# Matmul with bias and residual: the head loaded in smaller alternating pieces, the tail stored in another order

## The chip, the cores and the metric

The kernel runs on one core of a Trainium2 chip. A core has a matrix engine (TensorE, "PE" in the profile; its weight loads are "PEld"), VectorE ("DVE"), ScalarE ("ACT"), GpSimd ("POOL") and SyncE ("SP"), which here only issues transfers. Sixteen DMA engines move data between the device memory and the on-chip memory. The metric is the device time of one execution in microseconds (us). Before the change it is 211.38 us (median of 7 runs, 211.16 to 211.61). Profile times count from the span's start.

## The reference

```python
def setup_inputs():
    batch, m, k, n = 16, 512, 1024, 768
    # all standard normal, float32
    # x (batch, m, k), weight (k, n), bias (n,), residual (batch, m, n)

def reference(x, weight, bias, residual):
    return (np.matmul(x, weight) + bias + residual).astype(np.float32)
```

There are 8192 rows. x is 33.6 MB, residual and output are 25.2 MB each, weight is 3.1 MB.

## The kernel before

**Tiles.** The 8192 rows are cut into 64 tiles t of 128 rows and 8 super tiles S of 8 tiles (`J = 8`). In a super tile, partition p holds eight consecutive rows of memory, one for each of its tiles; so a transfer of tiles j0 to j1 of S is 128 rows of (j1 - j0) x 4096 bytes for x, or (j1 - j0) x 3072 bytes for the residual and the output.

**Buffers.** x has two super tile buffers (`X_SLOTS`), so x of S may be loaded when the casts of S - 2 are done. The residual has four (`RO_SLOTS`); the result is formed in place in the residual's buffer and stored from there, so the residual of S may be loaded when the store of S - 4 has landed. The weight is staged in residual buffer 1, so the residual of S1 has to wait for the casts of the weight. The first six tiles use buffer 3 for interim sums (`TMP_SLOT`, `EARLY_END`), so the residual of S3 waits until GpSimd has added those.

**One tile.** ScalarE (in the head also VectorE) casts a tile of x to bf16 (line 146; 143 and 144 where two engines share a tile). TensorE transposes it, two bf16 values taken as one fp32 word (line 154), VectorE copies the transposed tile out of PSUM (line 155), and 16 matmuls of 512 or 256 columns (line 161) make 128 x 768 sums in one of three PSUM buffers (`HEAD`). VectorE adds the residual to them (line 196, `finish`). The bias has been added to the residual by GpSimd beforehand (line 186, `pool_adds`). For tiles 0 to 5 it is the other way round: VectorE adds the bias to the sums (line 192), and GpSimd adds that to the residual later (line 182).

**Order of the work.** All engines run their instructions in the order in which the program gives them (`keep_in_program_order`). `HEAD_ORDER` is the head up to tile 2. The main loop does, for t from 3 to 63: cast of t + 2, transposes and PSUM copy of t + 1, matmuls of t, finish of t - 1. On VectorE the copy of t + 2 thus stands behind the finish of t - 1, and the matmuls of t + 2 can't begin before either is done. `ADDS` is a list of preference for GpSimd: `pool_adds(upto)` goes through it and emits those with t up to `upto`, but stops at the first whose data isn't there yet in program order. For the given list the order comes out as 0, 1, 2, 3, 6, 4, 7, 5, 8, 9 and on by number.

**Transfers.** All transfers are issued by SyncE, on one queue, in the order of the list `ORDER`. An entry is (kind, S, j0, j1): x, w (weight), b (bias), r (residual), s (store), c (store of one column chunk of the last tile). `pump()` goes through the list and stops at an entry whose producers haven't been emitted; SyncE then waits at run time for what the entry depends on. Each transfer also uses one of eight semaphores in turn, so it waits for the landing of the transfer issued eight before it. An entry of kind s may carry a fifth number, at which it is cut by partitions into two transfers (`edges`, line 125); no entry of the list before has one. The end of the list:

```python
 ('r', 7, 0, 8), ('s', 4, 0, 8), ('s', 5, 0, 8), ('s', 6, 0, 8), ('s', 7, 0, 5), ('s', 7, 5, 7),
 ('c', 7, 7, 0), ('c', 7, 7, 1)]
```

**Tail.** The last tile's matmuls (line 255) go chunk by chunk, 512 columns and then 256, each in a PSUM buffer of its own, each added (line 259) and stored by itself.

Of the kernel before, what the change touches and what calls it, by code (L numbers as in the profile page):

```python
# [16 lines left out]
HEAD = 3  # L17
XT_N = 4
# [1 line left out]
WARM = 12  # L20
EARLY_END = 6
TMP_SLOT = {0: 3}
ADDS = [6, 0, 7, 8, 1, 9, 2, 10, 3, 11, 4, 12, 5, 13, 14, 15]
HEAD_ORDER = [('cast', 0, 'v'), ('cast', 1, 's'), ('tr', 0), ('tr', 1), ('wc', 0, 0, 's'), ('wc', 0, 1, 'g'),
# [5 lines left out]
ORDER = [('x', 0, 0, 2), ('w', 0, 0, 2), ('x', 0, 2, 4), ('w', 1, 0, 2), ('b', 0, 0, 0), ('w', 2, 0, 2),  # L30
# [6 lines left out]


@with_exitstack
def kernel(  # L40
# [8 lines left out]
    nc = tc.nc  # L49
# [4 lines left out]
    N = weight.shape[1]  # L54
# [3 lines left out]
    chunks = [(0, 512), (512, N - 512)]  # L58
# [9 lines left out]
    def fixed(pool, name, n, shape, dt):  # L68
        return [pool.tile(shape, dt, name=f"{name}", tag=f"{name}{i}", bufs=1) for i in range(n)]
# [4 lines left out]
    XT = fixed(sb, "xt", XT_N, [P, n_q, P, 2], BF16)  # L74
    PO = fixed(ps, "psum_o", HEAD, [P, N], FP32)
# [7 lines left out]
    K_ = tc.keep_in_program_order  # L83
# [5 lines left out]
    def pump():  # L89
        while queue:  # L90
            kind, S, j0, j1, *cut = queue[0]
            if kind == "c":
                need = [("outc", j1)]
            elif kind in ("w", "b"):
                need = []
            elif kind == "x":
                need = [("cast", J * (S - X_SLOTS) + j) for j in range(j0, j1)] if S >= X_SLOTS else []
            elif kind == "r":
                need = [("store", S - RO_SLOTS, j) for j in range(j0, j1)] if S >= RO_SLOTS else []
                if S == 1:  # L100
                    need = [("wcast", n_q - 1)]
                if S in TMP_SLOT.values():
                    need = [("add", t) for t in range(EARLY_END) if TMP_SLOT[t // J] == S]
            else:
                need = [("out", J * S + j) for j in range(j0, j1)]
            if not all(n in done for n in need):
                return
            queue.pop(0)
            if kind == "b":
                K_(nc.sync.dma_start(  # L110
                    out=bias_row.rearrange("(g p) n -> g p n", p=QUAD)[:, 0, :],
                    in_=bias[None, :].to_broadcast([P // QUAD, N]),
                ))
                continue
            if kind == "w":
                K_(nc.sync.dma_start(out=w_st[:, 2 * S + j0:2 * S + j1, :], in_=w_d[:, S, j0:j1, :]))  # L116
                continue
            if kind == "x":
                K_(nc.sync.dma_start(out=X[S % X_SLOTS][:, j0:j1, :], in_=x_d[S, :, j0:j1, :]))  # L119
            elif kind == "r":  # L120
                K_(nc.sync.dma_start(out=R[S % RO_SLOTS][:, j0:j1, :], in_=res_d[S, :, j0:j1, :]))
            else:
                n0, nl = (0, N) if kind == "s" else chunks[j1]
                j1 = j1 if kind == "s" else j0 + 1
                edges = [0, *cut, P]
                for p0, p1 in zip(edges, edges[1:]):
                    K_(nc.sync.dma_start(
                        out=out_d[S, p0:p1, j0:j1, n0:n0 + nl],
                        in_=R[S % RO_SLOTS][p0:p1, j0:j1, n0:n0 + nl],
                    ))  # L130
                done.update(("store", S, j) for j in range(j0, j1))
            done.update((kind, J * S + j) for j in range(j0, j1))

    def mark(*what):
        done.add(what)
        pump()
# [30 lines left out]
    def row(t, n0=0, nl=N):  # L167
        return R[t // J % RO_SLOTS][:, t % J, n0:n0 + nl]
# [3 lines left out]

    adds = list(ADDS) + list(range(max(ADDS) + 1, n_t))

# [32 lines left out]
    def bias_rows():  # L207
        K_(nc.vector.stream_shuffle(out=bias_sb, in_=bias_row, mask=[0] * QUAD))

    pump()  # L210
    for kind, *a in HEAD_ORDER:
        if kind == "bias":
# [10 lines left out]
        elif kind == "wc":  # L223
            q, e, eng = a
# [4 lines left out]
        else:  # L229
            for e in range(2):  # L230
                for n0, nl in chunks:
                    mm(a[0], n0, nl, a[1], e)
    pump()
    for t in range(HEAD - 1):
        if ("fin", t) not in done:
# [12 lines left out]
        finish(t - 1)  # L248
        pool_adds(t + 1)
    t = n_t - 1  # L250
    tail = [(PO[t % HEAD], 0, 512), (PO[(t - 2) % HEAD], 512, N - 512)]
    for p, n0, nl in tail:
        for q in range(n_q):
            for e in range(2):
                K_(nc.tensor.matmul(  # L255
                    p[:, 0:nl], lhsT=XT[t % XT_N][:, q, :, e], rhs=w_sb[:, q, e, n0:n0 + nl],
                    start=(q == 0 and e == 0), stop=(q == n_q - 1 and e == 1),
                ))
        K_(nc.vector.tensor_add(out=row(t, n0, nl), in0=p[:, 0:nl], in1=row(t, n0, nl)))  # L259
        mark("outc", chunks.index((n0, nl)))  # L260
    mark("out", t)
    pump()
    assert not queue, queue
# [30 lines left out]
```

## Time and profile before

| | us |
|---|---|
| median of 7 runs | 211.38 (211.16 to 211.61) |
| the profiled execution | 211.59 |
| its span, first to last instruction | 209.80 |
| PE busy | 201.5 (96%) |
| POOL busy | 116.1 (55%) |
| DVE busy | 104.7 (50%) |
| ACT busy | 67.7 (32%) |
| DMA engines, share of the main queue | 97.6% |
| moved in all | 87.24 MB, 416 GB/s on the mean |

How to read it: a busy time is that of one engine's instructions; the share is of the span. The DMA share is the mean over sixteen engines. The chain of waits is followed back from the last instruction to what released each step. A transfer has landed when all its parts have: its data is spread over the DMA engines, and each of these marks the end of its own part, so that a transfer of 128 rows leaves sixteen marks in the trace. Single DMA packets are recorded too, with start, duration and size. The granted TensorE clock was 0.998 over the span.

### The profile page before, as it was taken

The numbers are of one execution on the slowest core, as the hardware profiler recorded it, in microseconds if no ns is written. First come the engines' busy times: TensorE is split into PE (matmuls) and PEld (weight loads), VectorE is DVE, ScalarE is ACT, GpSimd is POOL, SyncE is SP. The second block draws the span as 40 slices with busy tenths as digits, with TensorE's granted clock in tenths as the row PEclk, the third lists the DMA queues.
The fourth block names the chain that finished last, engine by engine and source line by source line (L and its number), as shares of the span: only waits on it lengthen the run. The fifth ranks groups of instructions, "written<-read, shape, count | busy, mean of one in ns | idle before, by whom it ended". The sixth has DMA issues, their size and how long they took to land.

```text
span 209.8 us, 3119 instructions
## 1 busy us (share of the span) xinstructions
PE 201.5 (96%) x1298; PEld 129.8 (62%) x1298; DVE 104.7 (50%) x140; ACT 67.7 (32%) x69; POOL 116.1 (55%) x72
## 2 busy tenths in 40 slices
PE   7799997999999999999999999999999999999991
PEld 2455655666666666666666666666666666666651
DVE  0558542465275445455544554455455445544542
ACT  2444207060733053323432152330633133321000
POOL 2100099995278980199599702994069910699000
PEclk9999999999999999999999999999999999999999
DMA  6999999999999999999999999999999999999785
GB/s 243 425 424 435 427 416 443 449 406 414 460 440 401 417 445 434 401 475 394 439 444 433 433 408 431 420 453 409 450 422 440 419 422 439 431 436 423 322 378 231
DMA packets 5350, 87.24 MB, mean 416 GB/s; under 512 B 596, under 2 KB 724, under 8 KB 1496
## 3 DMA queue, kind: packets, MB, share of 16 engines
q1 hardware_dynamic: 5336, 87.05, 97.6%
q8 instruction: 10, 0.16, 0.3%
q14 instruction: 4, 0.03, 0.0%
HBM read 61.88 MB, written 25.17 MB: 415 GB/s over the span
## 4 chain that ended last, share of the span: by engine, by line
PE 82%; DMA 14%; ACT 1%; SPq 0%; DVE 0%; issue 0%; ACTq 0%
PE psum_o L161 69%; DMA x_tile<-in_x_dram 14%; PE pt L154 12%; PE psum_o L255 1%; ACT xb L146 1%; DVE ro L259 0%; SPq L116 0%; SPq L119 0%; ACTq L146 0%
## 5 line engine op out<-in xcount | busy, mean ns | idle before, releaser
L161 PE MATMUL psum_o<-w_sb,xt 128*128 128x512 bf16 x1008 | 174.0, 326 | 0.5 <-DVE xt L155 0.3
L161 PEld LDWEIGHTS <-xt 128*128 128x128 bf16 x1008 | 98.5, 98 | 59.2 <-DVE xt L155 0.7
L186 POOL TENSOR_TENSOR ro<-ro,bias_sb 128x768 f32<-128x768 f32 x58 | 103.3, 1824 | 53.8 <-DMA ro<-in_residual_dram 53.8
L146 ACT CAST xb<-x_tile 128x1024 bf16<-128x1024 f32 x60 | 61.3, 1044 | 113.8 <-PE pt L154 57.0
L155 DVE COPY xt<-pt 128x1024 bf16<-128x1024 bf16 x64 | 44.0, 690 | 77.1 <-PE pt L154 77.1
L196 DVE TENSOR_TENSOR ro<-psum_o,ro 128x768 f32<-128x768 f32 x57 | 54.1, 950 | 13.6 <-POOL ro L186 12.5
L154 PE MATMUL pt<-ident,xb 128*128 128x128 f32 x256 | 38.4, 274 | 2.4 <-ACT xb L146 1.3
L154 PEld LDWEIGHTS pt<-ident,xb 128*128 128x128 f32 x256 | 29.6, 140 | 11.3 <-ACT xb L146 2.0
L182 POOL TENSOR_TENSOR ro<-ro 128x768 f32<-128x768 f32 x6 | 10.7, 1808 | 18.5 <-DMA ro<-in_residual_dram 18.5
L192 DVE TENSOR_TENSOR ro<-psum_o,bias_sb 128x768 f32<-128x768 f32 x6 | 5.6, 948 | 0.0
L205 PE MATMUL psum_o<-warm 128*128 128x512 bf16 x12 | 4.2, 521 | 1.2 <-DVE warm_a L201 1.2
L226 ACT CAST w_sb<-ro 128x768 bf16<-128x768 f32 x4 | 3.3, 832 | 3.7 <-DMA ro<-in_weight_dram 3.7
L226 POOL CAST w_sb<-ro 128x768 bf16<-128x768 f32 x1 | 0.8, 824 | 5.3 <-DMA ro<-in_weight_dram 5.3
L205 PEld LDWEIGHTS <-warm 128*128 128x128 bf16 x12 | 1.4, 126 | 3.5 <-issue 1.9
L143 ACT CAST xb<-x_tile 128x512 bf16<-128x512 f32 x3 | 1.8, 617 | 3.4 <-PE psum_o L161 1.7
L146 DVE CAST xb<-x_tile 128x1024 bf16<-128x1024 f32 x1 | 0.7, 693 | 4.3 <-DMA x_tile<-in_x_dram 4.3
L255 PE MATMUL psum_o<-w_sb,xt 128*128 128x512 bf16 (+1 forms) x16 | 2.8, 326 | 0.0
L226 DVE CAST w_sb<-ro 128x768 bf16<-128x768 f32 x3 | 1.7, 557 | 2.0 <-DMA ro<-in_weight_dram 2.0
L144 DVE CAST xb<-x_tile 128x512 bf16<-128x512 f32 x3 | 1.2, 425 | 2.6 <-DMA x_tile<-in_x_dram 2.6
L255 PEld LDWEIGHTS <-xt 128*128 128x128 bf16 x16 | 1.6, 98 | 1.1
L220 PE MATMUL psum_o<-warm 128*128 128x512 bf16 x6 | 1.6, 379 | 0.0
L259 DVE TENSOR_TENSOR ro<-psum_o,ro 128x512 f32<-128x512 f32 (+1 forms) x2 | 1.1, 558 | 0.9 <-PE psum_o L255 0.8
(14 smaller groups left out, 5.1 us busy)
## 6 DMA issues: line engine op xcount, KB each, us to landing
x_tile<-in_x_dram SPq DMA_DIRECT2D x6, 4096.0 KB, 30.1
out_dram<-ro SPq DMA_DIRECT2D x7, 3072.0 KB, 28.2
ro<-in_residual_dram SPq DMA_DIRECT2D x6, 3072.0 KB, 21.4
x_tile<-in_x_dram SPq DMA_DIRECT2D x4, 1024.0 KB, 10.8
x_tile<-in_x_dram SPq DMA_DIRECT2D x2, 2048.0 KB, 25.2
ro<-in_residual_dram SPq DMA_DIRECT2D x2, 1920.0 KB, 19.2
ro<-in_weight_dram SPq DMA_DIRECT2D x4, 768.0 KB, 9.8
ro<-in_residual_dram SPq DMA_DIRECT2D x2, 1152.0 KB, 27.9
```

The source lines that it names most:

```text
L143: K_(nc.scalar.copy(out=dst[:, 0:K // 2], in_=src[:, 0:K // 2]))
L146: K_((nc.scalar.copy if how == "s" else nc.vector.tensor_copy)(out=dst, in_=src))
L154: K_(nc.tensor.transpose(out=pt[:, q, :], in_=words[:, ts(q, P)], identity=ident))
L155: K_(nc.vector.tensor_copy(out=XT[t % XT_N].rearrange("p q m e -> p (q m e)"), in_=pt.rearrange("p q m -> p (q m)").bitcast(BF16),))
L161: K_(nc.tensor.matmul(PO[t % HEAD][:, n0:n0 + nl], lhsT=XT[t % XT_N][:, q, :, e], rhs=w_sb[:, q, e, n0:n0 + nl], start=(q == 0 and e == 0) ...
L182: K_(nc.gpsimd.tensor_add(out=r, in0=r, in1=tmp(t)))
L186: K_(nc.gpsimd.tensor_add(out=r, in0=r, in1=bias_sb))
L192: K_(nc.vector.tensor_add(out=tmp(t), in0=p, in1=bias_sb))
L196: K_(nc.vector.tensor_add(out=row(t), in0=p, in1=row(t)))
L205: K_(nc.tensor.matmul(PO[0][:, 0:512], lhsT=warm[:, 0:P], rhs=warm, start=True, stop=True))
L226: K_(copy(out=w_sb[:, q, e, :], in_=w_st[:, 2 * q + e, :]))
L255: K_(nc.tensor.matmul(p[:, 0:nl], lhsT=XT[t % XT_N][:, q, :, e], rhs=w_sb[:, q, e, n0:n0 + nl], start=(q == 0 and e == 0), stop=(q == n_q ...
```

## The change

It edits the lists and, in two places, code that reads them.

- x of S1 is loaded in three pieces (tiles 0 to 1, 2 to 4, 5 to 7) instead of two (0 to 3, 4 to 7); the residuals of S0 and of S1 in three pieces each instead of two; the pieces alternate in another order. The first tile of S0's residual goes ahead of the last two tiles of S0's x.
- In the middle, x of S5 is issued before the store of S1, the stores of S1 and S2 follow one another before the residual of S5, and the store of S3 is issued before the residual of S6.
- The store of S6 stands before that of S5. Of S7, tiles 0 to 6 are stored as 0 to 3, 4 to 5 and 6 instead of 0 to 4 and 5 to 6; the store of tile 6 is cut at partition 108 into two transfers. With the two column chunks of tile 7, that are six transfers instead of four.
- `ADDS` is another list. The order on GpSimd comes out as 0, 1, 2, 3, 5, 6, 7, 4, 8, 9 and on by number.
- `LAST` names the column chunks of the last tile; it has the same two as before, and the PSUM buffers and shapes come out the same. Nothing else changes on TensorE, VectorE or ScalarE.

```diff
-ADDS = [6, 0, 7, 8, 1, 9, 2, 10, 3, 11, 4, 12, 5, 13, 14, 15]
+ADDS = [0, 2, 13, 9, 5, 14, 12, 8, 6, 11, 1, 3, 7, 4, 15, 10]
...
- ('w', 3, 0, 2), ('x', 0, 4, 6), ('x', 0, 6, 8), ('r', 0, 0, 5), ('x', 1, 0, 4), ('r', 0, 5, 8),
- ('r', 1, 0, 5), ('x', 1, 4, 8), ('x', 2, 0, 8), ('r', 1, 5, 8), ('r', 2, 0, 8), ('x', 3, 0, 8),
- ('s', 0, 0, 8), ('r', 3, 0, 8), ('x', 4, 0, 8), ('r', 4, 0, 8), ('s', 1, 0, 8), ('x', 5, 0, 8),
- ('r', 5, 0, 8), ('s', 2, 0, 8), ('x', 6, 0, 8), ('r', 6, 0, 8), ('s', 3, 0, 8), ('x', 7, 0, 8),
- ('r', 7, 0, 8), ('s', 4, 0, 8), ('s', 5, 0, 8), ('s', 6, 0, 8), ('s', 7, 0, 5), ('s', 7, 5, 7),
- ('c', 7, 7, 0), ('c', 7, 7, 1)]
+ ('w', 3, 0, 2), ('x', 0, 4, 6), ('r', 0, 0, 1), ('x', 0, 6, 8), ('r', 0, 1, 6), ('x', 1, 0, 2),
+ ('r', 0, 6, 8), ('x', 1, 2, 5), ('r', 1, 0, 3), ('r', 1, 3, 6), ('x', 1, 5, 8), ('x', 2, 0, 8),
+ ('r', 1, 6, 8), ('r', 2, 0, 8), ('x', 3, 0, 8), ('s', 0, 0, 8), ('r', 3, 0, 8), ('x', 4, 0, 8),
+ ('r', 4, 0, 8), ('x', 5, 0, 8), ('s', 1, 0, 8), ('s', 2, 0, 8), ('r', 5, 0, 8), ('x', 6, 0, 8),
+ ('s', 3, 0, 8), ('r', 6, 0, 8), ('x', 7, 0, 8), ('r', 7, 0, 8), ('s', 4, 0, 8), ('s', 6, 0, 8),
+ ('s', 5, 0, 8), ('s', 7, 0, 4), ('s', 7, 4, 6), ('s', 7, 6, 7, 108), ('c', 7, 7, 0),
+ ('c', 7, 7, 1)]
+LAST = [(0, 512), (512, 256)]
...
-                n0, nl = (0, N) if kind == "s" else chunks[j1]
+                n0, nl = (0, N) if kind == "s" else LAST[j1]
...
-    tail = [(PO[t % HEAD], 0, 512), (PO[(t - 2) % HEAD], 512, N - 512)]
-    for p, n0, nl in tail:
+    for i, (n0, nl) in enumerate(LAST):
+        p = PO[(t - 2 * (i % 2)) % HEAD][:, 512 * (i // 2):512 * (i // 2) + nl]
```

More of the change, by code (lines that the diff above doesn't have):

```diff
@@ L255 @@
                 K_(nc.tensor.matmul(
-                    p[:, 0:nl], lhsT=XT[t % XT_N][:, q, :, e], rhs=w_sb[:, q, e, n0:n0 + nl],
+                    p, lhsT=XT[t % XT_N][:, q, :, e], rhs=w_sb[:, q, e, n0:n0 + nl],
                     start=(q == 0 and e == 0), stop=(q == n_q - 1 and e == 1),
                 ))
-        K_(nc.vector.tensor_add(out=row(t, n0, nl), in0=p[:, 0:nl], in1=row(t, n0, nl)))
-        mark("outc", chunks.index((n0, nl)))
+        K_(nc.vector.tensor_add(out=row(t, n0, nl), in0=p, in1=row(t, n0, nl)))
+        mark("outc", i)
     mark("out", t)
```

## The prediction

> Names: S0 to S7 are the super tiles, t the 64 row tiles; x1 0:2 is "x of S1, tiles 0 and 1 of it", r a residual, s a store; c0 and c1 are the last tile's column chunks. Times are us from the start of the span.
>
> **What bounds the kernel now.** I read the chain of waits first:
>
> ```profile
> PE 82%; DMA 14%; ACT 1%; SPq 0%; DVE 0%; issue 0%; ACTq 0%
> ...
> 9.77 21.61 DMA x_tile<-in_x_dram
> ...
> 32.57 0.66 PE pt L154 x4
> ...
> 202.99 2.61 PE psum_o L255 x16
> 205.60 0.02 issue
> 205.62 0.42 DVE ro L259
> ```
>
> It says: TensorE waits for x1 0:4 (landed 31.37) and then never again; 57 tiles at 3.04. That reading makes every us won before 32.57 a us won. The table by stage says something else:
>
> ```profile
> core 0: us, PE busy (x) PEld busy (x) DVE busy (x) ACT busy (x) POOL busy (x), PEclk, DMA share, GB/s
> 1.70:31.40 29.70, 27.95 (x162) 16.00 (x160) 14.86 (x23) 9.57 (x13) 5.88 (x5) 1.00 1.01 417
> 31.40:180.00 148.60, 147.43 (x971) 97.20 (x972) 75.92 (x98) 53.77 (x53) 94.91 (x54) 1.00 1.01 430
> 180.00:195.00 15.00, 15.00 (x100) 9.86 (x99) 7.59 (x11) 3.40 (x4) 14.21 (x8) 1.00 1.00 430
> 195.00:200.00 5.00, 5.00 (x34) 3.29 (x33) 2.46 (x4) 0.00 (x0) 0.00 (x0) 1.00 0.71 302
> 200.00:204.50 4.50, 4.50 (x28) 2.56 (x27) 2.51 (x3) 0.00 (x0) 0.00 (x0) 1.00 0.91 384
> ```
>
> The 16 DMA engines are full (1.00) from 1.7 to 195, and 0.71 in 195 to 200. An average; so I went to the single packets and to the sixteen landing marks of each transfer. x0 6:8 landed between 20.01 and 20.40; of the next, r0 0:5, fifteen parts landed by 25.00 and one at 26.48. Between them a 16384 B packet of the second queue
>
> ```profile
> q8 instruction: 10, 0.16, 0.3%
> ```
>
> ran on one engine from 23.34 to 24.44. Ten such packets come, some 20 apart, and an engine that was hit stays behind, since nothing is idle to let it catch up. One engine was hit at 23.34 and again at 177.89: it ends s6 at 201.10 where the first ends at 197.13. I call it A; a second, X, hit at 197.68, is 0.29 ahead of it. Fourteen engines wait in 195 to 200 and at 204.5; A never does. Its last stretch, s7 0:5 4.56, s7 5:7 1.82, c0 0.67, c1 0.35, runs without a gap from 201.10 to 208.50, and the last landing is A's, 208.84. The other engines land c1 by 208.37, bound by its issue:
>
> ```profile
> 205.54 0.33 SPq L127 DMA_DIRECT2D out_dram<-ro  x1
> 206.08 0.33 SPq L127 DMA_DIRECT2D out_dram<-ro  x1
> ```
>
> So two chains end 0.47 apart: the compute chain at 208.37 and A's bytes at 208.84. The end is A's.
>
> **The change, part by part.**
>
> *Smaller head pieces, for TensorE.* Until x1 0:4 has landed, 11.41 MB pass (x0, weights, r0 0:5, itself); until x1 0:2 has, 10.76 MB will (x0, weights, r0 0:6, itself). 0.655 MB less, at 0.4287 MB/us (38.92 MB landed in 31.37 to 122.15), is 1.53: it lands at 29.84. Cast 1.05, transposes at 31.04 for 32.57. They could start no earlier than 31.06 (matmuls of t6: 28.46 + 2.76 - 0.16). So the stall of 1.5 goes. What is late next: r0 1:6 lands 0.393 MB later than r0 0:5 did, 26.48 + 0.92 = 27.40. GpSimd adds tile 0 beforehand, and then, with the new ADDS, 1, 2, 3, 5, 6 (before: 0, 1, 2, 3, 6). The row:
>
> ```profile
> 26.62 7.12 POOL L182 TENSOR_TENSOR ro<-ro 128x768 f32<-128x768 f32 x4 [18.47 <-DMA ro<-in_residual_dram]
> 34.24 1.81 POOL L186 TENSOR_TENSOR ro<-ro,bias_sb 128x768 f32<-128x768 f32 x1 [0.49 <-DMA ro<-in_residual_dram]
> ...
> 36.08 0.96 DVE L196 TENSOR_TENSOR ro<-psum_o,ro 128x768 f32<-128x768 f32 x1 [2.13 <-POOL ro L186]
> 36.96 0.68 DVE L155 COPY xt<-pt 128x1024 bf16<-128x1024 bf16 x1
> ```
>
> 27.54 + 3 x 1.78 + 2 x 1.81 = 36.5; VectorE's finish of tile 6 (0.96) and, queued behind it, the copy of tile 9 (0.68) end at 38.1; matmuls of t9 at 38.25 where they began at 39.14. TensorE keeps 0.89. Nothing later eats more: x1 2:5 lands 35.4, cast by 36.5, wanted 37.4; x1 5:8 44.6, 45.7, wanted 47.1; x2 (0.39 MB later) 54.3, 55.4, wanted 56.2. r5 and r6 now stand behind one store more (3.15 MB, 7.3): they land at 137.06 and 161.3; with add 1.81, finish 0.96 and copy 0.68 the copies of tiles 43 and 51 end at 140.7 and 165.0, wanted 141.7 and 166.1. The last store is issued at 205.2 instead of 206.08. Bounds of TensorE's part: 0 and -1.5.
>
> *SP's queue.* A transfer also waits for the landing of the one eight issues earlier; more pieces mean fewer bytes in flight. x0 6:8 goes out at 7.3 (after w0) for 5.4, when 6.3 MB are queued to 17.9: no gap. r5 waits for s1's landing (122.4) while s2 fills the queue to 129.7; r6 for s2's, with x6, r5, s3 queued. s6 waits for tile 55 (issued 183.79 before, 182.9 now); six engines have drained s4 by 182.6 to 183.2 and idle up to 1.2, but they are the early ones; A ends s4 at 186.56. s5 goes right behind. s7 0:4 goes out at 195.0 (198.97 before): the idle of the fourteen goes, A had none. Cost for A: 0.
>
> *A's own bytes.* Same bytes, other packets. Per engine eight rows: 16384 B 4.89, 15360 B 4.59, 9216 B 2.79, 8192 B 2.48, 6144 B 1.85 (stores 1.82), 24576 B 7.27; 12288 B by interpolation 3.69 (store 3.65); 3072 B has the bias load's rows, 0.121 each, started 3 ns early: 0.118. r0: 0.95 + 4.60 + 1.85 for 4.60 + 2.79, +0.01; x1: 2.48 + 2 x 3.69 for 2 x 4.89, +0.08; r1: 2 x 2.79 + 1.85 for 4.59 + 2.79, +0.05. Head: +0.14 (bounds 0, the bytes alone, and 0.21, 0.07 fixed for each of three more transfers: 8192 B rows cost 2.48 where 16384 B rows cost 4.89).
>
> *The cut piece.* s7 6:7 is two stores, of 108 and 20 partitions. Two rows of this trace bear on it: 128 rows run on 16 engines, eight each; the bias load's 4 rows are four packets on four engines, with five landing marks for sixteen. Equal shares on the most engines that divide the rows would be 12 engines x 9 and 10 x 2: an estimate from those two rows. If both begin at the same engine, ten engines get 11 rows, two get 9, four get none. s7 0:7 then costs an engine 3.65 + 1.82 + 11 x 0.118 + 0.01 = 6.78 for 6.38: +0.40; with 9 rows +0.16; with none -0.91. Outer bounds: -0.91, and, by the bias row taken literally (four engines, 27 + 5 rows), 3.8 - 0.9 = +2.9 on those four; A carried none of the bias packets, so for A this end is excluded. I take +0.40: ten of sixteen engines, the nearer of the two rows being 128 on 16.
> The Trainium skill, "DMA: Bandwidth & Descriptors", "Why a DMA increments its semaphore by 16", says that a queue-issued transfer uses the largest number up to 16 that divides the slowest dimension, on the lowest-numbered engines; by it the three groups are the same, and A, without bias packet, would be above engine 3. The same page's "Rules for kernel authors" speaks against the change: at least 1 MiB a transfer, and don't split by partitions, with some 2 us fixed for each. Here 1.05 MB pieces landed 2.48 apart, the rate of the 4.19 MB ones, so in a full queue the fixed part does not show; by the rule five more transfers would mean up to 10 us, about 221.
>
> Sum for the end, A among the ten: +0.14 + 0.40 = +0.54, while the compute chain ends at 207.5 and is covered by A (if TensorE won nothing: 208.37, still covered). Span 209.80 to 210.34. The profiled run took 211.59, 1.79 more than its span and 0.21 over the median of 211.38: 211.38 + 0.54 = 211.92.
>
> **The rivals.**
> 1. A is among the two or the four, X among the ten: X ends at 208.61 + 0.54 = 209.15, +0.31: 211.69. Against: nothing in the trace; it is a matter of which engine.
> 2. Faster: A and X both in the group of four. A wins 0.91 - 0.14 = 0.77, 210.6; it decides if no engine within 0.8 of A carries the piece. The rest end s6 at 199.5 or before and have 1.6 of room; TensorE's 0.89 is then needed too, or 208.37 holds. For: A carried no bias packet, and engines hit in turn may be neighbours.
> 3. Faster: the late engine does not set the end (its second hit falls elsewhere, or it is quicker while others idle). Then the compute chain's 0.89 shows from 208.37: -1.3 at most, 210.1. Against: A's packets took 0.909 a row early and late alike.
> 4. The head pieces stall TensorE for over 1.5, or the cut piece sits on few engines: +1 to +2.9, 212.4 and more. Against: the slack listed.
>
> **How the numbers follow.** +0.2% or -0.2% (0.42) is about what a measurement of this kernel can tell from no change (runs spread 0.45). A among the ten: 0.47. Rival 1: 0.18. Rival 2: 0.21. Rival 3: 0.10. Rival 4: 0.04. Slower 0.51, within 0.18, faster 0.31. Signs are mixed, so the range runs from below rival 2 (210.6) to the forecast with its upper head bound, 212.1, and 0.2 of run spread: 210.4 to 212.3; rivals 3 and 4 are out. The forecast's own range: 211.7 to 212.1.
>
> **What would show it.** TensorE's transposes of t8 at 31.1 and t9's matmuls at 38.2, L255's end near 204.7; DMA share near 1.00 in 195 to 203; s6 issued at 183; last landing 209.3, on an engine with eleven 3072 B packets in the last pieces. Wrong if the latest engine has no 3072 B packets there, or if the last store's landing follows its issue by 2.3 on all engines.

## The result, and the profile after

The changed kernel is faster: 210.66 us (median of 13 runs, 210.56 to 211.04) against 211.29 us for the kernel before beside it, a ratio of 0.997 with a 95% interval of 0.9962 to 0.9977. That is 0.63 us less. The forecast was 211.92 us, slower; rival 2 said 210.6. The range of 210.4 to 212.3 holds the result, but only because it was drawn to reach below rival 2.

One caution on the traces. The execution of the changed kernel that was profiled first took 211.39 us, longer than each of the 13 timed ones. It serves below for the head and for TensorE. For the end of the run I use a second profiled execution of the same kernel, which took 210.70 us (span 208.9, where before had 209.8). What sets the first one apart is told at the end. The profiled execution of the kernel before took 211.59 us, 0.30 over the median beside the changed kernel; so differences between these two profiles come out larger (0.89) than those of the medians (0.63).

A correction to the text ahead of the prediction, which the prediction repeats: with the new `ADDS`, GpSimd's order is 0, 1, 2, 5, 6, 3, 7, 4, and not 0, 1, 2, 3, 5, 6, 7, 4. Tile 6's add still has three others between it and tile 0's, as before, and not four.

**The head.** First the chain of waits of the changed kernel (first execution), its shares and the stretch from 50 to 58 (start, length, what):

```profile
PE 71%; DMA 24%; ACT 1%; issue 1%; DVE 0%; SPq 0%; ACTq 0%
...
23.58 31.07 DMA x_tile<-in_x_dram
...
54.75 1.05 ACT xb L148
...
55.85 0.66 PE pt L156 x4
```

The last wait of TensorE is now for x of S2, which lands at 54.65, and no longer for x of S1 at 31.37. The timeline of TensorE and that of GpSimd (start, length, instruction, number; same execution) show what went:

```profile
28.57 2.76 PE L163 MATMUL psum_o<-w_sb,xt 128*128 128x512 bf16 x16
31.18 0.60 PE L156 MATMUL pt<-ident,xb 128*128 128x128 f32 x4
31.61 2.76 PE L163 MATMUL psum_o<-w_sb,xt 128*128 128x512 bf16 x16
34.21 0.60 PE L156 MATMUL pt<-ident,xb 128*128 128x128 f32 x4
34.65 2.76 PE L163 MATMUL psum_o<-w_sb,xt 128*128 128x512 bf16 x16
37.25 0.60 PE L156 MATMUL pt<-ident,xb 128*128 128x128 f32 x4
37.69 2.76 PE L163 MATMUL psum_o<-w_sb,xt 128*128 128x512 bf16 x16
```

```profile
27.41 5.36 POOL L184 TENSOR_TENSOR ro<-ro 128x768 f32<-128x768 f32 x3 [6.09 <-DVE ro L194]
32.73 1.81 POOL L188 TENSOR_TENSOR ro<-ro,bias_sb 128x768 f32<-128x768 f32 x1
34.50 1.82 POOL L184 TENSOR_TENSOR ro<-ro 128x768 f32<-128x768 f32 x1
```

Tile 9's matmuls before (the row stops at the end of the stretch that was asked for):

```profile
39.14 1.03 PE L161 MATMUL psum_o<-w_sb,xt 128*128 128x512 bf16 x5
```

The transposes of tile 8 begin at 31.18 (32.57 before). GpSimd's three adds of tiles 1, 2 and 5 are followed by tile 6's at 32.73, done at 34.54; so nothing waits for it, the matmuls of tile 9 begin at 37.69 (39.14 before), and TensorE is 1.45 ahead there. It is 1.59 ahead at the transposes of tile 15. Those of tile 16 wait for x of S2: TensorE idles for 0.22, and 0.43 of its lead is gone by tile 17.

```profile
201.83 2.62 PE psum_o L257 x16
```

The last matmuls begin at 201.83 (202.99 before): TensorE keeps 1.16. In the second execution it keeps 0.99.

**The end.** Busy time by stage in the second execution (columns as in the table shown of before):

```profile
core 0: us, PE busy (x) PEld busy (x) DVE busy (x) ACT busy (x) POOL busy (x), PEclk, DMA share, GB/s
180.00:195.00 15.00, 14.89 (x99) 9.84 (x100) 7.78 (x10) 3.14 (x3) 13.91 (x8) 1.00 0.99 423
195.00:200.00 5.00, 4.95 (x34) 3.42 (x34) 2.12 (x3) 0.00 (x0) 0.00 (x0) 1.00 0.96 406
200.00:204.50 4.50, 4.50 (x29) 2.55 (x26) 2.62 (x4) 0.00 (x0) 0.00 (x0) 1.00 0.97 400
```

```profile
204.55 0.89 SPq L129 DMA_DIRECT2D out_dram<-ro  x2
```

The DMA engines are 0.96 busy from 195 to 200, where it was 0.71. SyncE issues the two column chunks from 204.55 on, c1 at 205.08 (206.08 before). And the landing marks of the last transfers, the latest mark of each, which the rest of this document turns on:

| us | before | changed (second execution) |
|---|---|---|
| second of the two big stores (S6; S5) | 201.53 | 201.38 |
| first piece of S7 (0:5; 0:4) | 206.07 | 205.00 |
| next (5:7; 4:6) | 207.92 | 206.85 |
| tile 6, 108 rows, then 20 rows | (in 5:7) | 206.65, 206.88 |
| c0 | 208.51 | 207.54 |
| c1, the last | 208.84 | 207.86 |

The 108-row store has no mark near 207.8, where one would stand if the latest engine, done with 4:6 at 206.85, had carried eight or nine rows of it. It carried none: 206.85 + 0.69 = 207.54, + 0.32 = 207.86. The single packets say the same: the latest engine ends its last row of 4:6 at 206.46 (its mark follows some 0.4 later), and no packet of 3072 B, the size of tile 6's rows, starts after 206.28. Before, its share of tiles 0 to 6 took it 4.54 + 1.85 = 6.39; now its share of tiles 0 to 5 takes 3.62 + 1.85 = 5.47. That is 0.92 of the 0.98 by which the last landing comes earlier.

### The profile page after: what moved, and what is told of

The parts are those of the page before. It is cut to its first block, busy times and chain, and to the rows that moved or that the text cites. A ratio compares the mean times of both kernels' runs of the same rounds, so it can differ in the third digit from the quotient of the medians.

```text
span 209.6 us, 3125 instructions
## 1 busy us (share of the span) xinstructions
PE 201.7 (96%) x1298; PEld 130.0 (62%) x1298; DVE 105.0 (50%) x140; ACT 67.4 (32%) x69; POOL 116.1 (55%) x72
## 4 chain that ended last, share of the span: by engine, by line
PE 71%; DMA 24%; ACT 1%; issue 1%; DVE 0%; SPq 0%; ACTq 0%
PE psum_o L163 60%; DMA x_tile<-in_x_dram 22%; PE pt L156 10%; DMA ro<-in_weight_dram 3%; PE psum_o L257 1%; ACT xb L148 1%; DVE ro L261 0%; SPq L121 0%; ACTq L148 0%
```

## The experiments

The theory after the result was: the end is the later of two chains, (1) the bytes of the latest DMA engines and (2) the compute chain, from TensorE to the last store's issue and its landing (before: issued at 206.08, landed by 208.37 but for the two latest engines); the cut takes tile 6 off the late engines and the head pulls the compute chain in, and both are needed. Rivals: the head alone does it; the order of S6 and S5, or of the middle, does it; the late engine doesn't matter. Each ratio is against the kernel before beside it on the same chip.

### Head alone and tail alone

`e1_head` is the kernel before with the new `ADDS` and the new head of `ORDER`, and nothing of the middle or the tail.

```diff
-ADDS = [6, 0, 7, 8, 1, 9, 2, 10, 3, 11, 4, 12, 5, 13, 14, 15]
+ADDS = [0, 2, 13, 9, 5, 14, 12, 8, 6, 11, 1, 3, 7, 4, 15, 10]
...
- ('x', 0, 6, 8), ('r', 0, 0, 5), ('x', 1, 0, 4), ('r', 0, 5, 8), ('r', 1, 0, 5), ('x', 1, 4, 8),
- ('x', 2, 0, 8), ('r', 1, 5, 8),
+ ('r', 0, 0, 1), ('x', 0, 6, 8), ('r', 0, 1, 6), ('x', 1, 0, 2), ('r', 0, 6, 8), ('x', 1, 2, 5),
+ ('r', 1, 0, 3), ('r', 1, 3, 6), ('x', 1, 5, 8), ('x', 2, 0, 8), ('r', 1, 6, 8),
```

> The kernel before with the new head alone (pieces of S0's residual, S1's x and residual, and ADDS); middle and tail as before. Theory 1, the recorded one (the end is set by the bytes of the latest DMA engine): TensorE ends about 1.2 us earlier as in the profile after, but the end moves by the head's extra packets only, +0.1 to +0.2 us, ratio 1.0005 to 1.001. Theory 2 (in most executions no engine is that late and the end follows the compute chain): the 1.2 us of TensorE show, -0.5 to -1.2 us, ratio 0.994 to 0.998. Theory 3 (the gain is in the tail's stores alone): 0, ratio 0.9995 to 1.0005.

`e2_tail` is the kernel before with the new tail alone.

```diff
- ('s', 5, 0, 8), ('s', 6, 0, 8), ('s', 7, 0, 5), ('s', 7, 5, 7),
+ ('s', 6, 0, 8), ('s', 5, 0, 8), ('s', 7, 0, 4), ('s', 7, 4, 6), ('s', 7, 6, 7, 108),
```

> The kernel before with the new tail alone (S6 stored before S5, S7 in 0:4, 4:6, and 6:7 cut at partition 108). Theory 1: the late engine has nine rows where it had eight, +0.16 us, ratio 1.0008; with the late engine relieved -0.9 us, 0.996. Theory 2: TensorE ends as before, so nothing is won beyond 0.1 us, ratio 0.9995 to 1.001. Theory 3: most of the change's -0.63 us, ratio 0.997.

Measured: head alone 211.07 us, 0.9982 (0.9973 to 0.9991); tail alone 211.23 us, 0.9993 (0.9984 to 1.0002). SyncE's issue of the last store, head alone and then tail alone (there the line holds c0 and c1):

```profile
204.69 0.37 SPq L121 DMA_DIRECT2D out_dram<-ro  x1
```

```profile
205.49 0.89 SPq L121 DMA_DIRECT2D out_dram<-ro  x2
```

With the head alone c1 is issued 1.4 earlier than before (204.69), but only fourteen engines profit: thirteen marks of c1 lie by 206.95, one at 207.65, and the two latest at 208.18 and 208.19, at the end of 207.26 (tile 6), 207.88 (c0). Chain (1) holds the end. With the tail alone c1 is issued at 206.02, and its marks lie from 207.75 to 208.54, no single engine standing apart; the two late engines are done with 4:6 at 206.72 and 207.28, and the latest marks of the cut stores are 207.40 and 207.39, so neither late engine carried rows. Chain (2) holds the end. By its bytes the latest engine would be done near 208.3 (207.28 + 0.69 + 0.32). The halves measure 0.18% and 0.07%, the whole 0.30%. The tail alone is clear of the whole; the interval of the head alone just touches the whole's (0.9973 and 0.9977), so there it is the marks that show what is lacking. No range expected for the head alone holds its 0.9982: it was to cost 0.1 to 0.2 us with the late engine at the end, and it gained 0.3, since in its trace the late engine itself comes earlier (200.90 at S6's landing for 201.53; more on this below).

### The same test from the other side

`e8_delay` is the changed kernel (cut at 104, see below) with the head's gain taken away from TensorE alone: seven idle matmuls ahead of tile 8's.

```diff
+        if t == 8:
+            for _ in range(7):
+                K_(nc.tensor.matmul(PO[t % HEAD][:, 0:512], lhsT=warm[:, 0:P], rhs=warm, start=True, stop=True))
...
- ('s', 5, 0, 8), ('s', 7, 0, 4), ('s', 7, 4, 6), ('s', 7, 6, 7, 108), ('c', 7, 7, 0),
+ ('s', 5, 0, 8), ('s', 7, 0, 4), ('s', 7, 4, 6), ('s', 7, 6, 7, 104), ('c', 7, 7, 0),
```

> The changed kernel cut at 104, with seven idle matmuls of 512 columns (0.217 us each, 1.5 in all) in TensorE's queue before the matmuls of tile 8, which puts TensorE back to where it was before the change. Two chains: the late engine is relieved, so the end falls back to the compute chain, last store issued near 206.0 and landed by 208.4, ratio 0.998 to 0.9993. If the compute chain did not matter: 0.996. On the lateness that the new head took off (the last part of the sixth or fifth store landed at 200.9 to 201.2 with it, 201.5 and 201.8 without): if it follows TensorE's timing, this run has 201.5 or more; if it follows the pieces, 200.9 to 201.2.

Measured: 211.40 us, 0.9997 (0.9989 to 1.0006). Its timeline of TensorE, and SyncE's issue of the last stores:

```profile
31.65 2.76 PE L163 MATMUL psum_o<-w_sb,xt 128*128 128x512 bf16 x16
34.25 0.60 PE L156 MATMUL pt<-ident,xb 128*128 128x128 f32 x4
34.69 1.67 PE L247 MATMUL psum_o<-warm 128*128 128x512 bf16 x7
36.20 2.76 PE L163 MATMUL psum_o<-w_sb,xt 128*128 128x512 bf16 x15
```

```profile
205.49 0.36 SPq L129 DMA_DIRECT2D out_dram<-ro  x1
206.03 0.36 SPq L129 DMA_DIRECT2D out_dram<-ro  x1
```

Tile 8's matmuls begin 1.5 late (36.20), the last store goes out at 206.03, as before the change (206.08), and all sixteen marks of c1 lie between 207.77 and 208.39. Every transfer of the change is in it, only the cut stands at 104; the gain is gone. TensorE's microsecond won in the head is a condition of the gain. The run does not hold the late engines fixed, though: S6 is issued at 183.74 again and 4:6 lands at 207.21 at the latest, not at 206.44 or 206.77 as in the two runs at 104 below. With the 0.69 and 0.32 of c0 and c1 that engine would end near 208.2, so both chains have moved back.

### The cut of tile 6's store

`e3_uncut` is the changed kernel with tile 6 stored whole.

```diff
- ('s', 5, 0, 8), ('s', 7, 0, 4), ('s', 7, 4, 6), ('s', 7, 6, 7, 108), ('c', 7, 7, 0),
+ ('s', 5, 0, 8), ('s', 7, 0, 4), ('s', 7, 4, 6), ('s', 7, 6, 7), ('c', 7, 7, 0),
```

> The changed kernel with the store of tile 62 not cut at partition 108 (one store of 128 partitions). If the cut relieves the late engine (rival 2 of the prediction) the change's gain goes: ratio 1.000 to 1.001. If the late engine is among those with nine rows, as in the profile after, it is 0.15 us faster than the changed kernel, ratio 0.996. Theory 2: the same as the changed kernel within 0.1 us, ratio 0.9965 to 0.9975.

Measured: 211.18 us, 0.9993 (0.9984 to 1.0002). Against the changed kernel's 0.997 the cut is worth some 0.0023 of 211.3, 0.5 us. The latest engine's marks: 206.70 (4:6), 207.63 (tile 6), 208.26, 208.58. The eight rows of 3072 B that it now carries cost it 0.93.

Then the place of the cut. At 64 both halves are rows for all sixteen engines; 126 and 2 would be 14 engines of nine rows and two of one; 104 and 24 would be 13 of eight and 12 of two.

```diff
-('s', 7, 6, 7, 108)
+('s', 7, 6, 7, 64)
```

> The changed kernel with the store of tile 62 cut at partition 64: also two transfers, but each on all engines, four rows each. If the cut's gain is that four engines get no rows: it goes, ratio 0.9990 to 1.0000 as with no cut (0.9993). If two transfers instead of one are what helps: 0.997 as in the changed kernel.

```diff
-('s', 7, 6, 7, 108)
+('s', 7, 6, 7, 126)
```

> The changed kernel with the cut at partition 126: by equal shares 14 engines with 9 rows and two with one row more, two engines with none. If the late engines are the last two: as the changed kernel or 0.1 us faster, ratio 0.9965 to 0.9972. If one of them is among the two that now get nine rows: the gain goes, ratio 0.9993 to 1.0005.

```diff
-('s', 7, 6, 7, 108)
+('s', 7, 6, 7, 104)
```

> The changed kernel with the cut at partition 104: by the marks 13 engines with 8 rows and 12 of them with 2 more; the last three engines get none. The late engines are the 13th or 14th and the 15th. If the 14th: the gain stays, and the first ten engines have 10 rows for 11, ratio 0.9960 to 0.9970. If the 13th: it has eight rows, the gain goes, 0.999 to 1.000.

| cut at | ratio (95%) | latest marks: 4:6; first store; second store; c1 |
|---|---|---|
| none | 0.9993 (0.9984 to 1.0002) | 206.70; 207.63; -; 208.58 |
| 64 | 0.9986 (0.9975 to 0.9997) | 206.60; 207.10; 207.55; 208.51 |
| 126 | 0.9990 (0.9979 to 1.0001) | 206.45; 207.48; 205.69; 208.45 |
| 108 (the change) | 0.9970 (0.9962 to 0.9977) | 206.85; 206.65; 206.88; 207.86 |
| 104 | 0.9960 (0.9948 to 0.9972) | 206.44; 206.53; 206.77; 207.73 |

At 126 the latest engine goes from 206.45 to 207.48, nine rows in 1.03, and the gain is lost: its packets are nine of 3072 B without a gap, from 206.06 to 207.12. At 108 and at 104 it has none of tile 6. What pays is not that the store is cut but that the cut leaves the late engines out. The interval at 64 just touches that of the change (0.9975 and 0.9977); there the marks decide, with both halves on the latest engine (207.10, 207.55). Since 126 rows reach the latest engine and 104 do not, and the markers below give two candidates, it is the 14th of the sixteen in these executions.

Is 104 better than 108? Both were run once more, side by side:

> The changed kernel once more, beside the next two on one chip: ratio 0.9962 to 0.9977 again.

> The changed kernel cut at 104 once more: if ten rows for eleven on the first engines are worth the 0.12 us that one row takes, 0.1 to 0.2 us under the changed kernel beside it, ratio 0.9953 to 0.9968.

210.75 us, 0.9968 (0.9956 to 0.9980) for the changed kernel and 210.87 us, 0.9967 (0.9955 to 0.9979) at 104: no difference. The changed kernel already stands near a balance: in its second execution the latest mark of the cut stores, on an engine that carries rows of both, is 206.88, and 4:6's latest, on one that carries none, 206.85. Both then have the same c0 and c1 before them. In the second run at 104 the last landing (207.99) is that of an engine that carries rows of both stores (206.80, then 207.04).

### Which engines are late

To see which engine is late, small loads were put into the queue, right behind a store: each reads k rows of 64 B, for rising k. A load of k rows leaves k marks beside one that follows its issue at once, and the marks of 12 rows include those of 10, and so on. The k at which the late mark appears is the late engine's place. They add work and hold up the stores behind them (the kernels take 215.28 and 215.21 us), so their times don't count.

```diff
- ('r', 7, 0, 8), ('s', 4, 0, 8), ('s', 5, 0, 8), ('s', 6, 0, 8), ('s', 7, 0, 5), ('s', 7, 5, 7),
+ ('r', 7, 0, 8), ('s', 4, 0, 8), ('k', 0, 2, 0), ('k', 0, 4, 0), ('k', 0, 6, 0), ('k', 0, 8, 0),
+ ('k', 0, 10, 0), ('k', 0, 12, 0), ('k', 0, 14, 0), ('s', 5, 0, 8), ('s', 6, 0, 8), ('k', 0, 10, 0),
+ ('k', 0, 12, 0), ('k', 0, 14, 0), ('k', 0, 15, 0), ('s', 7, 0, 5), ('s', 7, 5, 7),
...
+            if kind == "k":
+                K_(nc.sync.dma_start(out=probes.pop()[0:j0, :], in_=x2d[0:j0, 0:16]))
+                continue
```

> The kernel before with small marker loads of k rows of 64 B (k = 2, 4, 6, 8, 10, 12, 14 behind the store of S4, k = 10, 12, 14, 15 behind that of S6). A load of k rows leaves k landing marks, one of each engine that it uses; a mark that lands over 1 us after the others is a late engine's. Theory 'the late engines are in the group of four that the cut leaves out': no late mark up to k = 12, late marks at 14 or 15 or none at all. If an engine of the first ten is late, its mark shows at k = 10 and below. That the loads of k rows use the same first engines shows in late marks that stay once they have come as k grows.

> The changed kernel with the same marker loads behind the stores of S4 and S5. Same late engines as in the kernel before if the late ones are a matter of the program; other ones if they change from execution to execution (in the profile after the last engine had nine rows of the cut store, in that of the variant with S5 first both late ones had none).

Measured, the two latest marks of each (from the trace's landing marks):

```
                          p_before            p_after
behind s4, store itself   185.31, 186.78      last 186.55
  k = 10                  185.40, 185.92      185.56, 185.60
  k = 12                  185.59, 186.12      185.76, 185.78
  k = 14                  186.32, 186.93      185.97, 186.71
behind the next two,
  store itself            203.18, 204.89      202.94, 204.66
  k = 12                  203.28, 203.58      203.00, 203.35
  k = 14                  203.49, 203.78      203.21, 203.57
  k = 15                  203.99, 205.06      203.76, 204.83
```

Behind s4, after the ninth code fetch, the late engine appears between 12 and 14: the 13th or the 14th. Behind the next stores, after the tenth fetch, it appears at 15: the 15th. It is so in both kernels, in one execution of each. Both late engines are thus above the twelfth, and 108 and 20 rows (12 and 10 engines) go past them both; with the 14th from the cuts they are neighbours. The Trainium skill, "DMA: Bandwidth & Descriptors", "Why a DMA increments its semaphore by 16", says that such a transfer takes the largest number of engines up to 16 that divides its slowest dimension, the lowest-numbered ones. The runs agree: 108, 20, 104, 24, 126 and 2 rows left 12, 10, 13, 12, 14 and 2 marks beside the early one.

### Order of the stores, of the middle, and the size of S7's first piece

```diff
- ('r', 7, 0, 8), ('s', 4, 0, 8), ('s', 6, 0, 8), ('s', 5, 0, 8), ('s', 7, 0, 4),
+ ('r', 7, 0, 8), ('s', 4, 0, 8), ('s', 5, 0, 8), ('s', 6, 0, 8), ('s', 7, 0, 4),
```

> The changed kernel with S5 stored before S6 again. Theory 1 and 2: same as the changed kernel within 0.1 us (the late engine has no gap at that place in either order), ratio 0.9965 to 0.9975. If holding S5 back matters because it leaves the early engines idle up to 1.2 us at 183 and lets the late one pass them, the ratio rises to 0.999 or more.

```diff
- ('x', 5, 0, 8), ('s', 1, 0, 8), ('s', 2, 0, 8), ('r', 5, 0, 8), ('x', 6, 0, 8), ('s', 3, 0, 8), ('r', 6, 0, 8),
+ ('s', 1, 0, 8), ('x', 5, 0, 8), ('r', 5, 0, 8), ('s', 2, 0, 8), ('x', 6, 0, 8), ('r', 6, 0, 8), ('s', 3, 0, 8),
```

> The changed kernel with the middle of the list as before (x of S5 behind the store of S1, the residuals of S5 and S6 ahead of the stores of S2 and S3). All theories: no difference from the changed kernel, ratio 0.9965 to 0.9978; over 0.998 would mean that the order in the middle has a part.

S5 ahead of S6 as before: 210.84 us, 0.9975 (0.9966 to 0.9985). The middle as before: 210.73 us, 0.9969 (0.9958 to 0.9980). Neither differs from the changed kernel within the intervals; these two parts do nothing that the runs can see.

Next, the new head and the cut alone, with S7's first piece as before (tiles 0 to 4), at 108 and at 104:

```diff
- ('s', 5, 0, 8), ('s', 6, 0, 8), ('s', 7, 0, 5), ('s', 7, 5, 7),
+ ('s', 5, 0, 8), ('s', 6, 0, 8), ('s', 7, 0, 5), ('s', 7, 5, 6), ('s', 7, 6, 7, 108),
```

> The kernel before with the new head and, in the tail, only the cut (S7 as 0:5, 5:6 and 6:7 cut at 108; S5 before S6, middle as before). Theory 'two chains, the late engine and the compute chain, the end is the later': head and cut are all that counts, ratio 0.9965 to 0.9975 as the changed kernel. If the smaller first piece of S7 or the new middle has a part, 0.998 to 0.999.

> As the run with the new head and the cut alone, but cut at 104. Same reasoning as for the changed kernel cut at 104: 0.9960 to 0.9970 if the late engines are the 14th and the 15th.

Measured: 211.05 us, 0.9991 (0.9980 to 1.0003) and 210.76 us, 0.9976 (0.9965 to 0.9987). Stage 195 to 200 and SyncE in the first of these:

```profile
195.00:200.00 5.00, 4.95 (x34) 3.41 (x34) 2.46 (x4) 0.00 (x0) 0.00 (x0) 1.00 0.91 386
```

```profile
197.64 7.66 SPq L121 DMA_DIRECT2D out_dram<-ro  x6
```

S7's first piece needs tile 4 and goes out at 197.64 instead of 194.94, and the DMA engines are 0.91 busy there, where the changed kernel had 0.96. The late engines have no rows of tile 6 here either (206.58 after tile 5), but engines that carry rows of both stores end at 207.09, 207.73 (c0) and 208.06 (c1). Both runs miss what was expected for head and cut alone. So the smaller first piece seems to have a part: it would give the early engines work in time, so that they can take the late engines' share. That is read from one trace and not shown: at 108 the intervals (0.9980 to 1.0003; 0.9962 to 0.9977) miss each other by 0.0003, at 104 they overlap, and the runs at 108 spread more than the others (210.74 to 212.05).

## Why the prediction was wrong

**What bounds the kernel: right.** Two chains, the compute chain and the late engine's bytes, with A last before the change. Head alone and tail alone gave what two chains give: the end stays with the other one. With the added matmuls the compute chain is back, and so is the time.

**The step that failed: "I take +0.40: ten of sixteen engines, the nearer of the two rows being 128 on 16."** The mechanism and the sizes were there: ten engines of 11 rows, two of 9, four of none, at 0.118 a row (nine rows 1.03 measured for 1.06, eight 0.93 for 0.94). What was wrong is that A's group was drawn by headcount, as if A were any engine. It was not: by the markers A is the 13th or 14th, X the 15th, and by the cuts the latest is the 14th; both are in the group of four, the one that the prediction prices at -0.91. (These are other executions than the one that it read; in that trace the place of A can't be seen.) The text held what spoke for this (A carried no bias packet, engines may be hit in turn as neighbours) under rival 2 and gave it 0.21. On the trace of before alone the place of A was open from 5 to 16; four of these twelve have no rows, and the second engine's place was tied to the first by a guess. So rival 2 deserved more than 0.21, but the trace did not settle it; the marker loads did. It is not a matter of the program alone either: in the first profiled execution of the changed kernel the latest engine was in the group of two, and that one took 211.39 us, no faster than before. All 13 timed ones came out at 211.04 or less.

**Rival 2's price was near.** It gave A -0.91 + 0.14 = -0.77, and 210.6; measured 210.66, and 0.92 saved on the pieces of S7. Beside the kernel before on one chip it is -0.63, and the cut alone is worth 0.5 end to end. It also said that TensorE's gain is then needed; the tail alone and the added matmuls bear that out.

**TensorE's part: the mechanism right, the size wrong.** The transposes of tile 8 came at 31.18 (forecast 31.04 to 31.1). "TensorE keeps 0.89" measured 1.45 at tile 9: the step had four adds between tile 0's and tile 6's on GpSimd, and there are three (27.41 to 32.73; tile 0's was out of the way at 21.3, as forecast). "x2 54.3, 55.4, wanted 56.2" measured 54.65 landed and 55.80 cast; with TensorE further ahead it was wanted at 55.63 or sooner, and 0.43 went back. Kept to the end: 1.16. The last store went out at 204.97 and 205.08 (forecast 205.2).

**SP's queue: right.** S6 was issued at 182.6 to 182.8 (forecast 182.9), S7 0:4 at 194.8 to 194.9 (195.0), r5 and r6 caused no wait on TensorE, and the new order of the stores cost nothing (`e4_s5first`). "The idle of the fourteen goes" holds: 0.71 to 0.96.

**"A's head packets +0.14": right where it was formed, and the other way later.** At the landing of the residual of S2 the latest mark is 63.56 on the mean of the three profiled executions with the old head (before, tail alone, markers before) and 63.74 on that of the fourteen with the new one: +0.18. At the residual of S7, behind the ninth fetch, it is 179.69 to 179.96 with the old head and 179.10 to 179.56 with the new one, and at the store of S4 186.85 and 186.58 on the mean, 0.3 earlier, though these last ranges overlap (186.76 to 187.02; 186.39 to 186.89). No step of the prediction has that. It is about what the head alone gains: 0.30 between the medians (its profiled execution, the fastest of its eleven, shows 0.65 at the last landing).

It does not follow TensorE: with TensorE delayed again (`e8_delay`) the two marks are 179.25 and 186.58, as with the new head. The expectation of that run set 201.5 or more at the second big store as the sign that TensorE's timing decides, and the latest mark there is 201.78. But by the packets that mark, like the 201.81 of the tail alone, belongs to the engine struck by the tenth fetch. The engine struck by the ninth ends its rows there at 200.66, and at 201.11 before, 200.83 (tail alone), 200.46 (head alone), 200.49 and 200.96 (changed kernel). So as far as these traces go it goes with the pieces of the head and not with TensorE's timing; by what way is not shown. In the changed kernel's second execution the earlier end of the second big store is 0.15 of 0.98, and `e3_uncut` has 0.31 of it at 0.9993; so the cut remains the larger term.

**The Trainium skill's "Rules for kernel authors"** ("DMA: Bandwidth & Descriptors"), at least 1 MiB a transfer and no split by partitions, spoke against the change. For two halves the runs agree: cut at 64 the ratio is 0.9986, uncut 0.9993, no difference within the intervals. For 108 and 20 partitions they go the other way: a store of 0.39 MB is what wins 0.5 us, since the split chooses the engines. The 2 us that the prediction takes with these rules stand elsewhere on the page, as a fit to transfers issued by GpSimd; here SyncE issues all of them.

## What to carry to other kernels

When the DMA engines are full to the end, look at the latest landing mark of the last transfers, engine by engine, before the mean share: one late engine can set the end alone, and a transfer whose partition count is not a multiple of 16 leaves some engines out, the smaller groups of engines being part of the larger ones (here 12 at 108, 13 at 104, 14 at 126). Such a cut pays only if the compute chain ends early enough as well, and only where the late engine is among those left out, which in one of the two profiled executions of this kernel it was not. Delay one chain to see the other. And where the sign of a forecast hangs on which of sixteen engines is meant, don't count heads: a few small transfers of rising row count behind the store in question tell it.

## What was not expected of the hardware

Code fetches cost the data queue real time. The page of the changed kernel has the same row as before:

```profile
q8 instruction: 10, 0.16, 0.3%
```

Ten packets of 16384 B in 209 us look like nothing, but each strikes one engine, and that engine fell 1.48 (before) or 1.21 and 1.64 (changed kernel twice, r0 1:6) behind the others at the first; behind s4, after the ninth, the latest is still 1.3 to 1.8 behind the next. At the ninth fetch of the kernel before, the packet itself holds its engine for 1.03, and the data packet of 24576 B behind it takes 1.28, where the usual one takes 0.91. The Trainium skill, "Runtime: NRT & Kernel Launch", "Instruction fetch mechanics", has the 16 KiB blocks and a DMA queue for them, and calls the fetch hidden; TensorE shows none of it here (its tiles keep their 3.04 us), while the struck engine's data was late by that much.

The place of the latest engine is not the same in each execution. In the first profiled execution of the changed kernel the latest engine was done with 4:6 at 206.55, and the store of 108 rows has a mark at 207.56, 1.01 later: it carried nine rows, but none of the 20-row store (latest 206.80), so it was the 11th or the 12th. By its packets it is the engine that the tenth fetch struck, which was the 15th in the marker runs. That execution's last landing is 208.54 and it took 211.39, 0.69 more than the second. Why the fetch struck another engine there stays open.
